# A float32 hybrid decoder layer: order of evacuations, unscaled first products, early output projection, bank-by-bank last tiles, 16-blocks in the triangular inverses

## The chip, the cores and the metric

One core of a Trainium2 chip. The metric is the device time of one launch in microseconds (us); the kernel before takes 2114.07 us (median of three runs, 2109.13 to 2115.06). Engine names are those of the profile: PE (TensorE, matrix products into PSUM), PEld (its weight loads), DVE (VectorE), ACT (ScalarE), POOL (GpSimd), SP (SyncE, which here only issues DMAs). Each engine, and each queue of DMA issues, works its instructions off in the order of the program.

## The reference

One layer on x (1024 tokens, width 1024, float32), three sub-layers with residuals and a norm at the end:

```
x = x + 0.5 * swiglu(rmsnorm(x, g1), w1, w3, w2)        # width 2816: (silu(h@w1) * (h@w3)) @ w2
p = rmsnorm(x, gm) @ w_in                               # 1024 -> 2816
y_rwkv = rwkv7(p[:, :1792])     # 8 heads x 64: S = S*diag(decay) + (S a) b^T + v k^T ;  y = S r
y_gmlp = gelu(pu) * (tril(w_s) @ layernorm(gelu(pv)) + b)  # chunks of 128 tokens
x = x + concat(y_rwkv, y_gmlp) @ w_out
x = x + 0.5 * swiglu(rmsnorm(x, g2), ffn2 weights)
out = rmsnorm(x, gf)
```

rmsnorm divides each token's row by the root of its mean square, then multiplies by a gain per channel. In the rwkv branch b is kk*a, where kk is the key divided by its norm over a head. The recurrence is computed in chunks of 64 tokens; a chunk needs the inverse of a unit triangular 64x64 matrix per head.

## The kernel before, in words

Everything is held transposed: channels on the 128 partitions, 512 tokens (one "row" or "half", 0 and 1) on the free axis. A float32 product is three products of 128x512 on operands that were split into a rounded part and the rest: an ACT cast (L740, L262, L500, L501) and a subtraction on DVE or POOL (L743, L263, L502, L503). The two feed-forward layers use Strassen's scheme of seven products. For the first product, `first_half` (L331) multiplies row 0 (tiles xt) by 22 column tiles of the weights (s = 0 to 21, 24 products each, in two parts); after part 0 the bank is copied out as an intermediate (L352), after part 1 it goes to `gate` (silu, product). `x_build` (L286) makes the combined operands xc from both rows while `first_half` runs; then `up` runs five further products, and `down` (L478) the seven of the third matrix, with `add` (L519, L521) adding each finished PSUM bank into the residual rows rd and res.

A norm's factor per token needs the whole row: `squares` sums squares over the channels, `spread` (L237) has PE sum over partitions, takes the power on POOL, and lets PE spread the factor over the partitions. `apply` (L270) multiplies the row by gain and factor and splits it into xt.

The mixer lies between about 700 and 1435 us. The main stream on PE is w_in, the gmlp part and w_out, one half of the tokens after the other. The rwkv branch is woven into it by `Flow`, which counts a planned time forward with each matrix product and lets a task go on when the planned time has come (`yield 3.0` is a pause of 3 planned us). Per half there are four `pair` tasks (elementwise work of two heads) and four `Oct` objects of 128 tokens (8 octs in all): `prep` (masked score matrices SC), `invert` (inverses of the 8x8 diagonal blocks on DVE, with relayouts through DRAM: ldr, M, tdr, T), `merge` (three levels, blocks of 8, 16, 32 joined by small PE products T,SC / T,X / X,T), `chain` (the state) and `finish`. After the first half's w_out, the second layer's `first_half` starts; at its step 12, or when the rwkv branch is through, `second` (L684) waits for the second half's rwkv results and runs that half's w_out, its norm and then the rest of `first_half`.

The final order on each engine is made by a scheduler that simulates the program; `hp` and `evac` raise priorities in it, and `add_manual_dep` with NoSync adds an order without a wait. Weight tiles go through four buffers raw and four buffers wsp.

Of the kernel before, what the change touches and what calls it, by code (L numbers as in the profile page):

```python
# [45 lines left out]
CON = [("ident", 128), ("me", 128), ("m8", 32), ("m16", 32), ("m32", 32), ("bo", 128), ("cm", 256), ("tri", 128)]  # L46
# [7 lines left out]
def host_constants():  # L54
# [10 lines left out]
        **{f"m{b}": (s64 // (2 * b) == t32 // b) & (s64 // b % 2 == 1) for b in (8, 16, 32)},  # L65
# [82 lines left out]
class K:  # L148
    def __init__(self, ctx, tc, a, out):
# [12 lines left out]
        self.edge = None  # L162
# [28 lines left out]

    def mm(self, *args, **kw):
        i = self.nc.tensor.matmul(*args, **kw)  # L193
        if self.edge is not None:
# [42 lines left out]
    def spread(self, acc, which, wait=1.6):  # L237
# [3 lines left out]
        for kk in range(2):  # L241
            for t in range(4):
                self.rmm(ps[:, t:t + 1], lhsT=sq[:, kk, t * P:(t + 1) * P], rhs=self.one,
                         start=(kk == 0 and t == 0), stop=(kk == 1), skip_group_check=True)
# [25 lines left out]
    def apply(self, dst, res, gain, rb, out=None, ks=range(KT)):  # L270

        nc = self.nc
        for k in ks:
            t = self.xtp.tile([P, HALF], F32, name="silu", bufs=3)
            nc.vector.scalar_tensor_tensor(t, res[k // 2][:, k % 2], self.v(gain, k), rb, op0=ALU.mult, op1=ALU.mult)
# [10 lines left out]
    def x_build(self, pool, xc, src, gain, rb):  # L286
# [15 lines left out]
        for kk in range(4):  # L302
# [10 lines left out]
            yield 3.0  # L313
# [5 lines left out]
            yield 3.0  # L319
# [11 lines left out]
    def first_half(self, xc, ws, hook):  # L331
# [14 lines left out]
        def head(s):  # L346
            wt = self.w_cols(ws[s % 2], s // 2, nc.gpsimd if s % 2 else nc.vector)
            o = self.psum("d")
            yield from prod(wt, o, 0)
            with self.evac():  # L350
                t = new()
                nc.scalar.copy(t, o)  # L352
                nc.sync.dma_start(self.sd[s], t)
            return wt, o

        nxt = yield from head(0)
        for s in range(2 * NP):
            wt, o = nxt
            between = hook(s)
            if s + 1 < 2 * NP and between is None:  # L360
                nxt = yield from head(s + 1)
            yield from prod(wt, o, 1)
            self.gate(us, new, s, 11, o)
            if s % 2:
                nc.sync.dma_start(self.hd[1][s // 2], us.pop(11))
            if between is not None:
                yield from between
                nxt = yield from head(s + 1)
# [109 lines left out]
    def down(self, pool, w2, res, done, loads):  # L478
# [40 lines left out]
        def add(p, bank, row, k):  # L519
            rv = res[row][k // 2][:, k % 2]  # L520
            ve.scalar_tensor_tensor(rv, bank, 0.5, rv, op0=ALU.mult, op1=ALU.add)  # L521
            done(p, row, k)

        for p, y, new, outs in plan:
            if new:
                sets[y] = banks(y)
            for jj in range(NP):
# [18 lines left out]
        for e in late:  # L546
            with self.evac():
                add(*e)

    def build(self, src, gain, w, rb, stats, ready, early=False):  # L550
# [10 lines left out]
        yield from self.x_build(pool, self.xc, src, gain, rb)  # L561
# [25 lines left out]
    def program(self):  # L587
# [17 lines left out]
        rx, rb = yield from self.row_stats(pool, src, "d", 0)  # L605
        x12 = self.halves()
        rbs = []
        self.apply(x12, rx, "g1", rb, self.xn)
        cb.close()
# [5 lines left out]
        flow.spawn(self.build(src, "g1", w1, rbs, stats1, ("xb", 0)))  # L615
        yield from self.first_half(x12, w1, lambda s: None)
# [10 lines left out]
        def task(row):  # L627
            yield 1.0
            rb = yield from self.spread(accs[row], "d" if row == 0 else "e", 2.5)
            if row == 0:  # L630
                rb = self.keep(rb)
                xm[0] = self.halves()
                for k in range(KT):
                    self.apply(xm[0], res[0], "gm", rb, ks=[k])
# [34 lines left out]
        yield ("rwkv", 0)  # L669
        accs = ([], [])  # L670
        out0 = yield from self.w_out(0, xres, accs[0], (self.mp, "h", 3))
        rb = yield from self.spread(accs[0], "e")
        rbs2 = []
        x12 = self.halves()
        self.apply(x12, out0, "g2", rb, self.xn)
# [8 lines left out]
        def second():  # L684
            yield ("rwkv", 1)
            crp.close()
            cm.close()
            p1, c1 = self.open("p1")
            yield from self.w_out(1, xres, accs[1], (p1,))
# [5 lines left out]
            rb1 = yield from self.spread(accs[1], "e")  # L695
            c1.close()
            cxq.close()
            flow.spawn(self.build(xres[1], "g2", w2, rbs2, stats2, ("xb", 1), True))

        yield from self.first_half(x12, w2, hook)  # L700
# [6 lines left out]
        def out(row):  # L707
            yield 1.0
            rb = yield from self.spread(accs[row], "d" if row == 0 else "e", 1.6)
            yield 0.5  # L710
            if row == 0:
                rb = self.keep(rb, pool)
            for k in range(KT):
                with self.hp(0 if row == 0 else PR_EVAC):
                    rv = res[row][k // 2][:, k % 2]
                    nc.vector.scalar_tensor_tensor(rv, rv, self.v("gf", k), rb, op0=ALU.mult, op1=ALU.mult)  # L716
                    (nc.scalar if k % 2 else nc.sync).dma_start(ov[row, k // 2][:, k % 2], rv)
                if row == 0:
                    yield 1.4

        def done2(p, row, k):
            if k % 2 == 0:
                return
            if (row == 0 and (p == 2 or p == 6)) or (row == 1 and p == 7 and k >= 4) or (row == 1 and p == 4):
# [616 lines left out]
```

## Time and profile before

| what | us |
|---|---|
| median of three runs | 2114.07 |
| profiled execution, own time | 2114.52 |
| its span, first to last instruction | 2112.4 |
| PE busy | 1971.0 |
| PEld busy | 1613.1 |
| DVE busy | 1160.4 |
| POOL busy | 975.3 |
| ACT busy | 700.5 |

Busy PE time counts every product from its start to its modelled end; products overlap, so the distance between starts says what one costs. The stages: norm of x to 22 us, first layer's `first_half` and `up` to about 485, `down` to 699, mixer to 1435, second half's w_out to 1489, rest of the second layer.

### The profile page before, as it was taken

Reading aid. Unit: us, or ns where it says so; the run is one execution under the profiler, and the core shown is the slowest. Engines: PE = TensorE matmul, PEld = TensorE weight load, DVE = VectorE, ACT = ScalarE, POOL = GpSimd, SP = SyncE. Lnnn points to the kernel's source line nnn. Section 1 sums busy time; section 2 is a strip of 40 time slices with the busy share of each in tenths; the row PEclk is TensorE's granted clock in tenths of the full one; section 3 lists DMA queues with packets and bytes.
Section 4 is the critical chain, followed back from the end, with each engine's and each line's share of the span. In section 5 each row is a group of like instructions: output and inputs, shape, how many; then the busy total and the mean of one; then the engine's idle time right before and its main releaser. Section 6 shows DMA issues by size and latency. Waiting matters only on the chain. (4 is left out here: it accounts for less than half of the span.)

```text
span 2112.4 us, 34477 instructions
## 1 busy us (share of the span) xinstructions
PE 1971.0 (93%) x13408; PEld 1613.1 (76%) x13408; DVE 1160.4 (55%) x1645; ACT 700.5 (33%) x1205; POOL 975.3 (46%) x749
## 2 busy tenths in 40 slices
PE   6999999998998999999899898997899999999987
PEld 5787888887876778767788777876678888878866
DVE  6716666646658354445534344324756666655576
ACT  5433222223443443241312122233442222224432
POOL 3426665554555565353323133124455666545542
PEclk9999999999999999999999998998899999999998
DMA  8655444447644576553443455435654544476452
GB/s 284 237 165 170 169 159 160 159 149 275 195 151 139 194 242 212 130 203 106 149 132 98 118 157 177 118 126 188 212 175 162 170 168 159 136 264 193 141 178 101
DMA packets 235187, 360.34 MB, mean 171 GB/s; under 512 B 68240, under 2 KB 101008, under 8 KB 235024
## 3 DMA queue, kind: packets, MB, share of 16 engines
q1 hardware_dynamic: 181248, 342.43, 49.0%
q10 hardware_dynamic: 53776, 15.71, 3.2%
q8 instruction: 105, 1.72, 0.3%
q14 instruction: 58, 0.48, 0.1%
HBM read 260.53 MB, written 97.53 MB: 170 GB/s over the span
## 5 line engine op out<-in xcount | busy, mean ns | idle before, releaser
L193 PE MATMUL psd<-xt,wsp 128*128 128x512 f32 x1920 | 490.0, 412 | 12.4 <-ACT silu L352 3.9
L193 PEld LDWEIGHTS psd<-xt,wsp 128*128 128x128 f32 x1920 | 369.3, 196 | 107.2 <-DVE wsp L743 4.9
L743 POOL TENSOR_TENSOR wsp<-raw,wsp 128x512 fp32r<-128x512 f32 x170 | 228.9, 1367 | 363.2 <-ACT wsp L740 353.3
L193 PE MATMUL psd<-xc,wup 128*128 128x512 f32 x1584 | 374.8, 389 | 4.0 <-ACT wup L257 3.6
L193 PE MATMUL psd<-wsp 128*128 128x512 f32 x1440 | 342.6, 397 | 14.1 <-ACT wsp L501 9.5
L193 PEld LDWEIGHTS psd<-xc,wup 128*128 128x128 f32 x1584 | 297.0, 188 | 67.2 <-ACT wup L257 4.5
L193 PEld LDWEIGHTS psd<-wsp 128*128 128x128 f32 x1440 | 271.9, 191 | 77.1 <-ACT wsp L501 11.4
L503 POOL TENSOR_TENSOR wsp<-raw,wsp 128x512 fp32r<-128x512 f32 x154 | 230.1, 1498 | 215.6 <-ACT wsp L501 165.7
L193 PE MATMUL pse<-xc,wup 128*128 128x512 f32 x1056 | 254.4, 389 | 0.0
L258 POOL TENSOR_TENSOR wup<-wraw,wup 128x512 fp32r<-128x512 f32 x132 | 179.0, 1365 | 127.2 <-ACT wup L257 126.2
L193 PEld LDWEIGHTS pse<-xc,wup 128*128 128x128 f32 x1056 | 198.0, 188 | 41.5 <-ACT wup L257 0.5
L740 ACT CAST wsp<-raw 128x512 fp32r<-128x512 f32 x246 | 139.7, 617 | 150.1 <-PE psd L193 98.5
L502 DVE TENSOR_TENSOR wsp<-raw,wsp 128x512 fp32r<-128x512 f32 x110 | 104.9, 966 | 80.1 <-ACT wsp L500 79.9
L385 DVE TENSOR_TENSOR wt<-wraw 128x512 f32<-128x512 f32 x44 | 42.1, 958 | 183.1 <-DMA wraw<-in_ffn_w_dram 183.1
L257 ACT CAST wup<-wraw 128x512 fp32r<-128x512 f32 x132 | 81.3, 619 | 179.4 <-PE psd L193 109.7
L193 PE MATMUL pse<-wsp 128*128 128x512 f32 x396 | 110.1, 406 | 17.2 <-DVE wsp L502 12.7
L500 ACT CAST wsp<-raw 128x512 fp32r<-128x512 f32 x110 | 68.2, 620 | 165.8 <-PE psd L193 65.3
L193 PE MATMUL psc<-wsp 128*128 128x512 f32 x396 | 106.8, 399 | 0.0
L501 ACT CAST wsp<-raw 128x512 fp32r<-128x512 f32 x154 | 94.9, 617 | 32.4 <-DMA raw<-hd 25.7
L193 PEld LDWEIGHTS pse<-wsp 128*128 128x128 f32 x396 | 76.7, 196 | 36.7 <-DVE wsp L502 15.9
L743 DVE TENSOR_TENSOR wsp<-raw,wsp 128x512 fp32r<-128x512 f32 x76 | 60.4, 828 | 69.2 <-ACT wsp L740 56.5
L193 PEld LDWEIGHTS psc<-wsp 128*128 128x128 f32 x396 | 76.5, 194 | 16.4
(225 smaller groups left out, 2509.0 us busy)
## 6 DMA issues: line engine op xcount, KB each, us to landing
wraw<-in_ffn_w_dram SPq DMA_DIRECT2D x88, 512.0 KB, 4.6
raw<-hd SPq DMA_DIRECT2D x154, 256.0 KB, 3.5
raw<-in_ffn_w_dram SPq DMA_DIRECT2D x132, 256.0 KB, 3.2
raw<-in_ffn_w_dram SPq DMA_DIRECT2D x44, 512.0 KB, 4.3
raw<-in_w_in_dram SPq DMA_DIRECT2D x36, 512.0 KB, 4.1
hd<-u SPq DMA_DIRECT2D x66, 256.0 KB, 2.5
hd<-s SPq DMA_DIRECT2D x66, 256.0 KB, 5.0
sd<-silu SPq DMA_DIRECT2D x44, 256.0 KB, 3.4
```

The source lines that it names most:

```text
L193: i = self.nc.tensor.matmul(*args, **kw)
L257: nc.scalar.copy(t[:, 0], src)
L258: eng.tensor_tensor(t[:, 1], src, t[:, 0].bitcast(F32), op=ALU.subtract)
L385: ve.tensor_sub(t1, b12, b11)
L500: nc.scalar.copy(t[:, 0, 0], w)
L501: nc.scalar.copy(t[:, 0, 1], h)
L502: ve.tensor_tensor(t[:, 1, 0], w, t[:, 0, 0].bitcast(F32), op=ALU.subtract)
L503: ge.tensor_tensor(t[:, 1, 1], h, t[:, 0, 1].bitcast(F32), op=ALU.subtract)
L740: self.nc.scalar.copy(dst[:, 0, sl], src[:, sl])
L743: eng.tensor_tensor(dst[:, 1, sl], src[:, sl], dst[:, 0, sl].bitcast(F32), op=ALU.subtract)
```

## The change

1. **Start and first products.** `apply` can run without the factor (rb None). `first_half` runs three heads (part 0 of s = 0 to 2; two in the second layer) on rows that carry only the gain; then the factor comes, and the banks are multiplied by it on the way out: `keep` and the new `gate` multiply on DVE, and POOL multiplies silu's result once more. The scaled rows xn are made later, in `first_build` and `rows`.
2. **Order of evacuations.** `pace` ties an elementwise instruction behind the last main product that was issued; `add` uses it, and takes a bank's uses together.
3. **Early output projection.** `w_out` does its four gmlp tiles first and only then waits for rwkv; `hook` fires when the last chain is through (or at step 17), and the second half's norm and `build` run as a task beside `first_half`.
4. **Last tiles bank by bank.** In product 4 of `down` the last three operand tiles are held and run through one bank after the other; each bank is evacuated behind its own products, and `done2` sums squares tile by tile. Two of the eight last scalings go to POOL.
5. **Inverses from 16-blocks.** `invert` works on 64 partitions with two 8x8 blocks each, joins them to 16x16 on DVE, and `merge` has two levels. The norm of kk is taken per head and chunk (`inv`) and multiplied into SC and Bt; `spread2` and `back2` go.
6. **Relayout DMAs** (ldr, M, tdr, T) are issued by SP, before by ACT. `w_cols` alternates DVE and POOL for the split where POOL did all.

```
+    def pace(self, i):
+        self.tc.add_manual_dep(i.ins, self.last.name, ...NoSync...)
...
     def first_half(...)
+        for s in range(ahead):
+            q.append((yield from head(s)))
+        rb = self.keep((yield from stat))
+        self.flow.spawn(then(rb))
+        for s in range(ahead):
+            keep(s, q[s][1])
...
+        def keep(s, o):
+                nc.vector.tensor_mul(t, o, rb)
+        def gate(s, c):
+                if s % 2 == 0:
+                    nc.vector.tensor_mul(u, c, rb)
+                    nc.scalar.activation(u, u, AF.Silu)
+                    nc.gpsimd.tensor_tensor(u, u, rb, op=ALU.mult)
+                else:
+                    nc.vector.tensor_mul(u, u, c)
...
     def down(...)
-            ve.scalar_tensor_tensor(rv, bank, 0.5, rv, op0=ALU.mult, op1=ALU.add)
+            i = ve.scalar_tensor_tensor(rv, bank, 0.5, rv, op0=ALU.mult, op1=ALU.add)
+            if p != 4:
+                self.pace(i)
...
+                if p == 4 and jj >= NP - 3:
+                    held.append(t)
+                    continue
...
-            for o in outs:
-                for f in range(4):
+            for f in range(4):
+                for o in outs:
                     late.append(...)
+            if p == 4:
+                for f, e in enumerate(late):
+                    for jj, t in enumerate(held):
+                        (the three products of t into bank f)
+                    with self.evac():
+                        add(*e)
...
     def hook(s):
-            if state["done"] or not (("rwkv", 1) in flow.done or s >= 12):
+            if state["done"] or not (("chain", 2 * NO - 1) in flow.done or s >= 17):
...
     def w_out(...)
+                if hf == 0 and n == 4:
+                    yield ("rwkv", half)
+                    sums = ready()
...
     def invert(...)
-        M = self.tl("M", 1, (P, 8, 8))
-        nc.scalar.dma_start(M, self.diag(self.ldr))
+        M = self.tl("M", 1, (64, 16, 16))
+        nc.sync.dma_start(M, self.diag(self.ldr))
...
+        for l, r, o in ((D[:, 0, 0:8, 0:8], M[:, 0:8, 8:16], Z), (Z, D[:, 0, 8:16, 8:16], D[:, 0, 0:8, 8:16])):
+            nc.vector.tensor_mul(tv, l.unsqueeze(2).broadcast_to([64, 8, 8, 8]), ...)
+            nc.vector.tensor_reduce(o, tv, axis=AX.X, op=ALU.add)
...
     def merge(...)
-        for lvl, bs in enumerate((8, 16, 32)):
+        for lvl, bs in enumerate((16, 32)):
...
     def pair(...)
-        ss = self.spread2(sq)
+        for i in range(HALF // CH):
+            for s in HS:
+                self.rmm(ss[s, i:i + 1], lhsT=sq[s, i * CH:(i + 1) * CH], rhs=self.one[s], ...)
-        inv = self.back2(i8)
-        ve.tensor_mul(a, a, inv)
```

How instructions move, at three places. First DVE, where the first layer's `down` goes over from its first product to the next; dt and wsp are operands of coming products, rd and res are evacuations of finished banks. Before:

```order
L502 TENSOR_TENSOR wsp<-raw,wsp 128x512 x7
L493 TENSOR_TENSOR dt<-raw,dt 128x512
L502 TENSOR_TENSOR wsp<-dt,wsp 128x512
L521 SCALAR_TENSOR_TENSOR rd<-psd,rd 128x512 x4
L521 SCALAR_TENSOR_TENSOR res<-psd,res 128x512 x8
L493 TENSOR_TENSOR dt<-raw,dt 128x512 x4
L502 TENSOR_TENSOR wsp<-dt,wsp 128x512 x2
```

Now, with buffer numbers:

```order
L532 TENSOR_TENSOR dt_3816<-raw_4059,dt_3816 128x512
L532 TENSOR_TENSOR dt_3839<-raw_4084,dt_3839 128x512
L541 TENSOR_TENSOR wsp_4060<-dt_3816,wsp_4060 128x512
L560 SCALAR_TENSOR_TENSOR rd_3775<-psd_3781,rd_3775 128x512
L560 SCALAR_TENSOR_TENSOR res_3779<-psd_3781,res_3779 128x512
L560 SCALAR_TENSOR_TENSOR res_3777<-psd_3781,res_3777 128x512
L560 SCALAR_TENSOR_TENSOR rd_3775<-psd_3782,rd_3775 128x512
L532 TENSOR_TENSOR dt_3862<-raw_4107,dt_3862 128x512
L541 TENSOR_TENSOR wsp_4085<-dt_3839,wsp_4085 128x512
L532 TENSOR_TENSOR dt_3885<-raw_4130,dt_3885 128x512
L532 TENSOR_TENSOR dt_3908<-raw_4153,dt_3908 128x512
L560 SCALAR_TENSOR_TENSOR res_3779<-psd_3782,res_3779 128x512
```

Twelve evacuations stood in one block between two operands; now they come three or four at a time between the operands.

Second, PE at the second half's w_out (psd<-wsp) inside the second layer's `first_half` (psd<-xt,wsp); psd<-xc,wup is `up`, pse<-con,Y the last `finish`. Before:

```order
L193 MATMUL psd<-xt,wsp 128x512 x12
L202 MATMUL psc<-WA,SC 64x64 x8
L202 MATMUL pse<-con,Y 64x64 x16
L193 MATMUL psd<-wsp 128x512 x192
L202 MATMUL pse<-one,xs 128x1 x8
L202 MATMUL pse<-con,rr_r 128x128 x4
L193 MATMUL psd<-xt,wsp 128x512 x216
L193 MATMUL psd<-xc,wup 128x512 x2
```

Now:

```order
L200 MATMUL psd<-xt,wsp 128x512 x24
L200 MATMUL psd<-wsp 128x512 x5
L200 MATMUL psd<-xt,wsp 128x512 x12
L200 MATMUL psd<-wsp 128x512 x22
L210 MATMUL pse<-con,Y 64x64 x16
L200 MATMUL psd<-wsp 128x512 x162
L200 MATMUL psd<-xt,wsp 128x512 x3
L210 MATMUL pse<-one,xs 128x1 x8
L200 MATMUL psd<-xt,wsp 128x512 x9
L210 MATMUL pse<-con,rr_r 128x128 x4
L200 MATMUL psd<-xt,wsp 128x512 x108
L200 MATMUL psd<-xc,wup 128x512 x2
```

The last `finish` moves from ahead of w_out into it, and 120 products instead of 216 stand between w_out and `up`.

Third, the relayouts of the first oct. Before, on ACT, among casts and copies:

```order
L1143 DMA ldr_6874<-SC_6841 64x8x64 x2
L1172 DMA M_7045<-ldr_6874 128x8x8
L740 CAST wsp_6774<-raw_6772 128x512 x2
L1158 COPY Bt_6981<-pse_6964 128x512
L1187 DMA tdr0_0_5534<-D_7047 128x8x8
L1187 DMA tdr0_1_5536<-D_7047 128x8x8
L1158 COPY Kt_7000<-pse_6983 128x512
L1191 DMA T_7227<-tdr0_0_5534 64x8x64
L1158 COPY VV_7031<-pse_7014 128x512
L1191 DMA T_7227<-tdr0_0_5534 64x8x64
L1191 DMA T_7227<-tdr0_1_5536 64x8x64 x2
```

Now, on SP, among loads of weights (raw):

```order
L1279 DMA M_7113<-ldr_6989 64x16x16
L1212 DMA oB_7104<-xB0_135 128x4x128
L850 DMA raw_7090<-in_w_in_dram 128x1024
L1212 DMA oK_7106<-xK0_136 128x4x128
L1212 DMA oV_7108<-xV0_137 128x4x128
L1309 DMA tdr0_0_5572<-D_7115 64x16x16
L1309 DMA tdr0_1_5574<-D_7115 64x16x16
L1313 DMA T_7298<-tdr0_0_5572 64x8x64 x2
L1313 DMA T_7298<-tdr0_1_5574 64x8x64 x2
L1245 DMA ldr_7202<-SC_7166 64x8x64 x2
L850 DMA raw_7155<-in_w_in_dram 128x1024
```

The waits of the relayouts for DVE's D and for their own landings now stand in front of SP's loads.

## Rows read from the trace of the kernel before

**Rows 1.** two stretches: length, busy us (instructions) by engine, PEclk, DMA, GB/s
```profile
300.00:400.00 100.00, 100.00 (x443) 82.81 (x442) 59.67 (x82) 27.97 (x47) 61.18 (x46) 1.00 0.51 168
...
700.00:1435.00 735.00, 677.80 (x7839) 557.23 (x7840) 309.65 (x595) 219.27 (x389) 264.39 (x236) 0.94 0.50 151
```

**Rows 2.** PE's waits, whole span: us in total, times, longest
```profile
PE pse L193 <- DVE wsp L502: 12.7, 5, 4.6
PE psd L193 <- ACT wsp L501: 9.5, 4, 7.0
```

**Rows 3.** timeline, start: start, length, instruction, count, [idle before <-releaser]
```profile
4.60 1.06 ACT L231 ACTIVATE xs<-rx 128x1024 f32<-128x1024 f32 x1 [1.65 <-DMA rx<-in_x_dram]
...
21.86 0.62 ACT L262 CAST xt<-silu 128x512 fp32r<-128x512 f32 x1 [1.60 <-DVE silu L275]
...
22.53 4.29 PE L193 MATMUL psd<-xt,wsp 128*128 128x512 f32 x9 [1.49 <-DVE silu L275]
...
29.88 7.27 PE L193 MATMUL psd<-xt,wsp 128*128 128x512 f32 x21
...
37.80 10.52 PE L193 MATMUL psd<-xt,wsp 128*128 128x512 f32 x44
```

**Rows 4.** timeline, two places in the first `down`, one in the second
```profile
500.26 2.07 PE L193 MATMUL pse<-wsp 128*128 128x512 f32 x4 [4.53 <-ACT wsp L500]
...
671.47 27.88 PE L193 MATMUL psd<-wsp 128*128 128x512 f32 x108 [7.03 <-ACT wsp L501]
...
2049.71 1.22 PE L193 MATMUL pse<-wsp 128*128 128x512 f32 x2 [4.64 <-DVE wsp L502]
```

**Rows 5.** timeline, TensorE in the mixer: bursts of small products
```profile
820.21 1.09 PE L202 MATMUL pse<-con,i 128*64 128x128 f32 x16
...
870.60 1.12 PE L202 MATMUL pse<-T,SC 64*64 64x32 f32 x32
871.66 5.16 PE L193 MATMUL psd<-xt,wsp 128*128 128x512 f32 x21
876.75 1.12 PE L202 MATMUL pse<-T,X 64*64 64x32 f32 x32
877.70 1.10 PE L202 MATMUL pse<-X,T 64*64 64x32 f32 x32
```

**Rows 6.** mixer: DMA issues (KB, us to landing), then a wait of SP
```profile
T<-tdr ACTq DMA_DIRECT2D x32, 128.0 KB, 3.5
...
M<-ldr ACTq DMA_DIRECT2D x8, 32.0 KB, 2.8
...
SPq L747 <- POOL wsp L743: 100.0, 31, 12.1
```

**Rows 7.** timeline, from the mixer to the second `up`
```profile
1306.88 1.12 PE L202 MATMUL psc<-S,AR 64*64 64x64 f32 x16 [4.46 <-DVE WA L1245]
...
1433.34 1.98 PE L202 MATMUL pse<-con,Y 64*64 64x64 f32 x32 [8.43 <-POOL Y L1278]
...
1489.56 3.58 PE L202 MATMUL pse<-one,xs 128*128 128x1 f32 x16 [4.27 <-DVE xs L233]
...
1497.21 1.41 DVE L306 SCALAR_TENSOR_TENSOR nx<-nx,vec,rbk 128x512 f32<-128x512 f32 x2 [3.88 <-ACT rbk L283]
...
1505.27 0.68 DVE L263 TENSOR_TENSOR xc<-nx,xc 128x512 fp32r<-128x512 f32 x1
...
1506.47 1.78 DVE L263 TENSOR_TENSOR xc<-nx,xc 128x512 fp32r<-128x512 f32 x1
...
1535.24 1.28 POOL L263 TENSOR_TENSOR xc<-nx,xc 128x512 fp32r<-128x512 f32 x1 [1.28 <-ACT xc L262]
```

**Rows 8.** timeline, end of the span
```profile
2090.03 2.73 DVE L521 SCALAR_TENSOR_TENSOR rd<-psd,rd 128x512 f32<-128x512 f32 x4 [5.65 <-PE psd L193]
...
2096.29 3.57 PE L202 MATMUL pse<-one,xs 128*128 128x1 f32 x16 [4.26 <-DVE xs L233]
...
2103.32 5.36 DVE L716 SCALAR_TENSOR_TENSOR rd<-rd,vec,pse 128x512 f32<-128x512 f32 x8 [3.26 <-PE pse L202]
```

More of the change, by code (lines that the diff above doesn't have):

```diff
@@ L161, in __init__ @@
         self.ws = e(tc.tile_pool(name="ws", bufs=1, reuse_waits="tile"))
-        self.edge = None
+        self.edge = self.last = None
+        self.turns = 0
         base = self.base
@@ L235, in squares, with spread @@
                 acc.append(s)
-    def spread(self, acc, which, wait=1.6):
+    def spread(self, acc, which, wait=1.6, extra=None):
         sq = acc[0]
         ps = self.psum(which)
-        for kk in range(2):
+        parts = [sq[:, 0], sq[:, 1] if extra is None else extra]
+        for kk, x in enumerate(parts):
             for t in range(4):
-                self.rmm(ps[:, t:t + 1], lhsT=sq[:, kk, t * P:(t + 1) * P], rhs=self.one,
+                self.rmm(ps[:, t:t + 1], lhsT=x[:, t * P:(t + 1) * P], rhs=self.one,
                          start=(kk == 0 and t == 0), stop=(kk == 1), skip_group_check=True)
@@ L268, in halves, with apply @@
         return [self.xtp.tile([P, 2, 2, HALF], F32R, name="xt", bufs=4) for _ in range(4)]
-    def apply(self, dst, res, gain, rb, out=None, ks=range(KT)):
+    def apply(self, dst, res, gain, rb, out=None, ks=range(KT), pace=False):
         nc = self.nc
@@ L329, in gate, with first_half @@
                 nc.vector.tensor_mul(us[key], us[key], c)
-    def first_half(self, xc, ws, hook):
+    def first_half(self, xc, ws, hook, stat, then, ahead, wt0=None):
         nc = self.nc
@@ L604, in program, with first_build @@
         pool, cb = self.open("p0")
-        rx, rb = yield from self.row_stats(pool, src, "d", 0)
         x12 = self.halves()
-        rbs = []
-        self.apply(x12, rx, "g1", rb, self.xn)
-        cb.close()
+        rbs, acc0, rx, wt0 = [], [], [], None
+        for kp in range(4):
+            if kp == 2:
+                wt0 = self.w_cols(w1[0], 0, nc.vector)
+            t = pool.tile([P, 2, HALF], F32, name="rx", bufs=4)
+            nc.sync.dma_start(t, src[0][kp])
+            rx.append(t)
+            self.apply(x12, rx, "g1", None, ks=(2 * kp, 2 * kp + 1))
+            self.squares(pool, acc0, t)
+        def first_build(rb):
+            yield 20.0
+            for k in range(KT):
+                t = pool.tile([P, HALF], F32, name="nt", bufs=2)
+                nc.vector.scalar_tensor_tensor(t, rx[k // 2][:, k % 2], self.v("g1", k), rb, op0=ALU.mult, op1=ALU.mult)
+                nc.sync.dma_start(self.xn[k], t)
+                yield 3.0
+            cb.close()
+            yield from self.build(src, "g1", w1, rbs, stats1, ("xb", 0), pace=8.0)
         def stats1(pool):
@@ L693, in stats2 @@
                 rbs2.append(self.keep(rb1, pool))
[L695 to L700, printed above, removed]
+            yield from self.build(xres[1], "g2", w2, rbs2, stats2, ("xb", 1), True)
+        yield from self.first_half(x12, w2, hook, self.spread(accs[0], "e"), rows, 2)
         yield from self.rest(w2, ("xb", 1), cxt.close)
@@ L764, in dense_T, with w_out @@
         return o
-    def w_out(self, half, xres, acc, sums):
+    def w_out(self, half, xres, acc, ready, x12=None):
         nc = self.nc
@@ L830, in mixer_consts @@
         nc.gpsimd.memset(self.S, 0.0)
+        self.inv = [mp.tile([P, PR, HALF // CH], F32, name=f"inv{h}") for h in range(2)]
         self.pcc = [mp.tile([P, PR, HALF // CH], F32, name=f"pcc{h}") for h in range(2)]
@@ L1212, in merge @@
             pt = K_.psum("e", (P, 2, NB, CH // 2))
-            for n in range(1 if lvl == 2 else 2):
+            for n in range(1 if lvl == 1 else 2):
                 for b in range(NB):
```

237 lines of the change are left out of this document (152 added, 85 removed).

## The prediction

> **What bounds the kernel now.** I read stretches first, then PE's waits, then the timeline at each place where one ends. In the stretch from 300 to 400 us PE starts 443 products of 128x512, one per 0.226 us, and is busy all the time at a granted clock of 1.00 [rows 1]: there nothing but fewer products could help, and the change takes none of these away. In the mixer (700 to 1435) PE is still busy 677.8 of 735 us, but with 7839 instructions at a clock of 0.94 [rows 1]: many are small, and each removed one is time on the path. PE's waits name the rest: the products of `down` wait for operand splits, 12.7 and 9.5 us [rows 2]. The timeline then shows the start, two places of `down`, the mixer, the second w_out and the end [rows 3, 4, 5, 7, 8]. So the kernel is bound by PE, and the question is what each part takes from PE's stream or from its gaps.
>
> The sum is made against the profiled execution (2114.5 us, span 2112.4), which lies 0.45 us above the median: the same number for this purpose. By repetition 0.3%, 6 us, is what can be told from no change.
>
> **Start.** Before, the first products wait for the norm: 9 start at 22.53, 21 at 29.88, and the steady stream only at 37.80 (44 in 10.52 us, 0.239 each) [rows 3]. Now they need the gain alone, but the statistic queues behind other work: on ACT four squares of 1.06 and eight casts of 0.62 (rows and first weights) from 4.60 on, to about 13.8 [rows 3], then a DVE addition of 1024 columns (twice the 0.68 of 512 [rows 7]), so 15.1. The partition sums take 3.58 [rows 7] and the way from their start to the first use of the factor 7.0 (2096.29 to 2103.32 [rows 8]). In PE's order 46 products stand before the factor's spreading, 32 of them behind the sums: 18.7 + 32 x 0.226 = 26, or 33 if they run at half clock. With the second row's sums (3.6) 48 products are done by 30 to 37; before, the 48th starts at 37.80 + 18 x 0.239 = 42.1. Gain 5 to 12; I take 9, and keep 2 to 15, since evacuations now go over DVE and a POOL product.
>
> **Evacuations in `down`.** At 500.26, 671.47 and 2049.71 PE has waited 4.53, 7.03 and 4.64 us for a split [rows 4], each time because DVE had a block of evacuations or final scalings in front of the operand. The order rows show that block of twelve cut into threes and fours. Four-bank blocks remain at product 4 with fewer operands ahead, so I don't count all: of the 22.2 us of the two wait lines and the 4.5 of the first place [rows 2, 4] three quarters, 18 net of what shifts. Bounds 6 (only the first place) and 30 (all, with the slow products behind it).
>
> What such a wait costs is seen at 671.47: the 108 products behind it take 27.88 us, 3.5 more than 108 x 0.226 = 24.4 [rows 1, 4]. The Trainium skill (TensorE: Matmul & The Clock Gate, HAM oscillation) says that an idle gap throttles the array and that what follows runs cold; by that rule the trace agrees, and a removed 7 us gap would be worth 10.5. My sum leaves this out except in the bound of 30.
>
> **Mixer, products removed.** One merge level per oct goes: T,SC, T,X and X,T, 32 instructions each. Start to start such a burst costs 1.06 (870.60 to 871.66) and 0.95 (876.75 to 877.70) [rows 5], so 3.0 per oct and 24 for eight. `back2` was 16 instructions per pair, 820.21 to about 821.2, 1.0 each: 8 for eight pairs. `spread2`'s eight are replaced by 32 of one column per pair; the trace has no such product, the nearest are the 32 of 32 columns at 1.0. I take old and new as equal. Together 32. Bounds: 12, if most of the freed time turns into waiting for the recurrence, and 45, if waits inside the bursts go too. What is added lies on DVE: per oct two products and two reductions of 512 elements, at 0.68 each 2.7 us [rows 7], against a DVE that is busy 309.65 of 735 [rows 1]; a merge level with its two evacuations is taken out of the same latency. At nothing, as long as DVE's idle half covers it.
>
> **Relayouts on SP.** ACT loses waits, SP gets them. SP then stands per oct until ldr has landed (about 2.8, as M), M has (2.8), D is there (some 6 of DVE by the row lengths above), tdr and T follow (about 3 and 3.5) [rows 6]: an estimate of 15 us in which a weight load behind it doesn't go out. Four raw buffers cover that: the mixer loads 82 weight tiles in 735 us (five rows of the DMA issues there, 35 + 13 + 24 + 8 + 2), 9 us each, so 36 us of stock, and SP's longest wait is for buffers to come free (100.0 us in 31 times [rows 6]), so it is ahead. I take -4 (ACT's casts come earlier), bounds -15 and +20.
>
> **Second w_out.** Three gaps of PE: 4.46 behind the first half's w_out, with DVE at applying the factor (now applied late), 8.43 for the last `finish` (now inside w_out), 4.27 for the sum of squares [rows 7]. Of the last 0.7 is covered by the three products ahead of it, the others go: -13. Against it stands the build of xc. It ran from 1497.21 to 1535.24 + 1.28, 39.3 us, under 216 products [rows 7]; now 120 stand between w_out and `up`. From w_out's last product PE comes to `up` after 120 x 0.226 + 3.6 of wait + 3.6 of sums + about 2 of spreading = 36; the build begins after 3.6 + 0.7 + 7.0 = 11 and ends at 50, its first-needed operands some 4 sooner. So PE waits about 10: bounds 0 and 20. Sum for this place: -3.
>
> **End.** Before: last additions from 2090.03 for 2.73, the sums 2096.29, the scalings 2103.32 for 5.36 [rows 8]. Now three banks are added and squared under the next bank's products; behind the last there is one addition (0.68), half a square and half of the sums (1.8 saved), and six scalings instead of eight (1.3 saved). From the last addition to the sums 3.5 shrink to about 0.6: 2.9 + 1.8 + 1.3 = 6, bounds 3 and 8.
>
> **Sum.** 9 + 18 + 32 + 4 + 3 + 6 = 72 less: 2114.5 - 72 = 2042.5, so 2043 us.
>
> **Rivals.**
> *The freed mixer time isn't returned.* The recurrence goes oct by oct, and `invert` has longer planned pauses (7, 2, 9 for 4, 2.4 and 6). Against it: the main stream has no tie to the octs until w_out, and PE's idle share is small there [rows 1]. With 12 of 32 returned and DVE as the later releaser, 2063 to 2075.
> *DVE and POOL hold each other up in the two `first_half`.* A subtraction takes 0.68 and, beside POOL, 1.78 [rows 7]; new are a DVE evacuation and POOL's product per two steps. If the second build takes ten more and evacuations hold the banks, 15 to 25 on top: 2058 to 2068. The Trainium skill (SBUF — State Buffer, Who interferes with whom) gives the rule: a DVE instruction with two SBUF inputs and a reading GpSimd one exclude each other, one with a single SBUF input doesn't contend. By it the new evacuations (one input from PSUM) stay free and only the build's additions suffer; the 1.78 agrees.
> *More than counted.* All gaps of `down` go with their slow tails (30), the waits in the merges too (45), and the build is in time: 12 + 13 + 10 further, about 2005 to 2015.
> *Slower: SP runs dry.* If SP stands over 36 us per oct, because D waits in DVE's queue and T's landing behind it, weight loads come too late and PE stops: beyond that point 12 to 15 us for each of eight octs, some 110 against 72 gained: about 2150. For it: the second oct's ldr already stands in front of a load in the order rows. Against: the estimate of 15.
> *The parts do nothing*, since `down` and the build find new waits as large: 2110.
>
> **How the numbers follow.** Forecast 0.53 (own range 2023 to 2063), time not returned 0.16, DVE and POOL 0.10, more than counted 0.13, SP dry 0.05, nothing 0.03. The range 2003 to 2088 holds all of the first three and most of the fourth, over 8 in 10. Faster by over 0.3%: 0.92 less a small part for surprises in these, 0.91; within: 0.03; slower: 0.06.
>
> **What would show it.** Steady products before 30 us; no wait over 3 us of PE for a split of `down`; 256 instructions less in T,SC and T,X each and in X,T, with the mixer about 30 us shorter; no wait before pse<-con,Y but one before the first psd<-xc,wup; last product to end of span about 15 us instead of 20. I am wrong if PE's busy time falls but its idle time grows by as much, or if SP's waits for D and T are followed by PE waits for weights.

## The result

The changed kernel takes 2098.03 us (median of five runs, 2096.19 to 2104.43), the kernel before 2111.25 (five runs beside it). The ratio is 0.9934, 95% interval 0.9912 to 0.9957: faster by 13 to 14 us, where 72 were forecast. The profiled execution has a span of 2095.0 us against 2112.4.

By the first product of each stage on PE (where `up` goes over into `down`, by the last product of `up`), and the clock of the whole execution:

| stretch of the profile, us | before | after | difference | forecast |
|---|---|---|---|---|
| start to the first `up` | 160.9 | 167.2 | +6.3 | -9 |
| first `up` | 302.2 | 303.6 | +1.4 | 0 |
| first `down` | 239.5 | 240.7 | +1.2 | -18 for both |
| mixer, w_out, `first_half` to the second `up` | 855.4 | 838.0 | -17.4 | -39 |
| second `up` | 302.1 | 305.0 | +2.9 | 0 |
| second `down` | 231.5 | 223.7 | -7.8 | see above |
| its last product to the end of the span | 20.7 | 16.8 | -3.9 | -6 |

```profile
core 0: 2112.4 us, clock 0.962
```

for the span and mean granted clock before, and after:

```profile
core 0: 2095.0 us, clock 0.953
```

### The profile page after: what moved, and what is told of

Same layout as the page of the kernel before. It is cut to its first block, busy times and chain, and to the rows that moved or that the text cites. A ratio compares the mean times of both kernels' runs of the same rounds, so it can differ in the third digit from the quotient of the medians.

```text
span 2095.0 us, 33201 instructions
## 1 busy us (share of the span) xinstructions
PE 1937.4 (92%) x12704; PEld 1587.4 (76%) x12704; DVE 1281.4 (61%) x1819; ACT 677.3 (32%) x1159; POOL 977.4 (47%) x736
## 5 line engine op out<-in xcount | busy, mean ns | idle before, releaser
L200 PE MATMUL psd<-xt,wsp 128*128 128x512 f32 x1920 | 494.3, 415 | 36.9 <-DVE silu L372 16.8
L200 PEld LDWEIGHTS psd<-xt,wsp 128*128 128x128 f32 x1920 | 376.5, 200 | 126.9 <-DVE silu L372 13.1
L542 POOL TENSOR_TENSOR wsp<-raw,wsp 128x512 fp32r<-128x512 f32 x154 | 232.1, 1514 | 192.3 <-ACT wsp L540 157.7
L846 POOL TENSOR_TENSOR wsp<-raw,wsp 128x512 fp32r<-128x512 f32 x134 | 187.5, 1415 | 251.0 <-ACT wsp L843 250.7
L541 DVE TENSOR_TENSOR wsp<-raw,wsp 128x512 fp32r<-128x512 f32 x110 | 107.3, 986 | 58.1 <-ACT wsp L539 57.8
L846 DVE TENSOR_TENSOR wsp<-raw,wsp 128x512 fp32r<-128x512 f32 x112 | 93.9, 871 | 56.1 <-ACT wsp L843 55.9
L200 PE MATMUL pse<-wsp 128*128 128x512 f32 x396 | 105.3, 393 | 3.1 <-DVE wsp L541 2.6
L540 ACT CAST wsp<-raw 128x512 fp32r<-128x512 f32 x154 | 94.8, 617 | 16.8 <-DMA raw<-hd 14.7
L200 PEld LDWEIGHTS pse<-wsp 128*128 128x128 f32 x396 | 73.2, 188 | 22.2 <-DVE wsp L541 6.5
```

Of the source, the lines that this page charges most:

```text
L540: nc.scalar.copy(t[:, 0, 1], h)
L541: ve.tensor_tensor(t[:, 1, 0], w, t[:, 0, 0].bitcast(F32), op=ALU.subtract)
L542: ge.tensor_tensor(t[:, 1, 1], h, t[:, 0, 1].bitcast(F32), op=ALU.subtract)
L846: eng.tensor_tensor(dst[:, 1, sl], src[:, sl], dst[:, 0, sl].bitcast(F32), op=ALU.subtract)
```

## The profile after

**The start** came as forecast. TensorE's timeline of the changed kernel (start, length, instruction, count, [idle before <-releaser]), to answer [rows 3]:

```profile
10.10 1.22 PE L200 MATMUL psd<-xt,wsp 128*128 128x512 f32 x2 [10.10 <-ACT wsp L843]
12.34 5.49 PE L200 MATMUL psd<-xt,wsp 128*128 128x512 f32 x12 [1.02 <-DVE wsp L846]
20.52 2.65 PE L210 MATMUL pse<-one,xs 128*128 128x1 f32 x16 [2.69 <-DVE xs L241]
23.03 10.06 PE L200 MATMUL psd<-xt,wsp 128*128 128x512 f32 x32
...
33.74 0.71 PE L200 MATMUL psd<-xt,wsp 128*128 128x512 f32 x2
34.29 1.84 PE L210 MATMUL pse<-one,xs 128*128 128x1 f32 x16
```

The 48th product is done at 34.5 and the second row's sums at 36.1, where before the 48th ended at 42.1 (37.80 + 18 x 0.239 [rows 3]): 6 to 8 us gained, 9 forecast.

**It is lost again before `up`.** The stretch from the first product to the first `up`, with length, busy us (instructions) of PE, PEld, DVE, ACT, POOL, granted clock, DMA share, GB/s. Before:

```profile
22.00:161.00 139.00, 133.87 (x553) 107.00 (x553) 77.44 (x91) 62.08 (x113) 55.14 (x39) 0.99 0.62 205
```

and after:

```profile
10.00:167.00 157.00, 138.30 (x576) 110.64 (x576) 112.72 (x135) 57.58 (x97) 77.31 (x52) 0.95 0.63 214
```

DVE is busy 35 us more, POOL 22 more, PE idle 19 us instead of 5, and the clock is 0.95 instead of 0.99. What PE waits for, in the whole span (us in total, times, longest), to answer [rows 2]:

```profile
PE psd L200 <- DVE silu L372: 16.8, 6, 6.7
PE psd L200 <- ACT wsp L843: 15.4, 2, 10.1
PE psd L200 <- ACT wup L266: 12.8, 2, 11.0
PE pse L210 <- DVE oG L1408: 12.0, 3, 5.9
PE psd L200 <- ACT wsp L540: 10.4, 4, 5.0
```

The first line is `keep`, the evacuation that now multiplies by the factor. The kernel before waits once for its copy on ACT, 3.9 us in the second layer, and never in the first. Here is the longest one of the first layer, on all engines' timeline:

```profile
155.40 0.69 DVE L424 TENSOR_TENSOR wt<-wraw 128x512 f32<-128x512 f32 x1 [5.96 <-DMA wraw<-in_ffn_w_dram]
156.01 0.68 DVE L384 TENSOR_TENSOR silu<-silu,psd 128x512 f32<-128x512 f32 x1
...
159.49 0.68 DVE L372 TENSOR_TENSOR silu<-psd,rbk 128x512 f32<-128x512 f32 x1
160.09 0.68 DVE L424 TENSOR_TENSOR wt<-wraw 128x512 f32<-128x512 f32 x1
160.32 5.13 PE L200 MATMUL psd<-xt,wsp 128*128 128x512 f32 x12 [6.18 <-DVE silu L372]
```

DVE stands 5.96 us for a weight load of `up`; the evacuation that holds the bank is queued behind it and five more instructions. DVE had such a wait before too (5.4 us for the same load), but the copies then stood in ACT's queue, and PE waited for none of them there. And the twelve products behind the gap take 5.13 us, 0.43 each instead of 0.226 [rows 1]: the granted clock from 160 to 165 us is 0.51, the lower of its two levels (1.2 and 2.4 GHz).

**The second `first_half`**, with w_out inside it, waits for the last `finish`, for a bank and for the build of xc:

```profile
1454.48 1.98 ACT L843 CAST wsp<-raw 128x512 fp32r<-128x512 f32 x3 [3.93 <-DMA raw<-yr]
1455.15 34.53 PE L200 MATMUL psd<-wsp 128*128 128x512 f32 x144 [5.30 <-ACT wsp L843]
...
1529.07 5.15 PE L200 MATMUL psd<-xt,wsp 128*128 128x512 f32 x12 [6.68 <-DVE silu L372]
...
1549.44 1.22 PE L200 MATMUL psd<-xc,wup 128*128 128x512 f32 x2 [11.04 <-ACT wup L266]
```

The result of `finish` comes back through DRAM (tile yr), so moving `finish` into w_out turned 8.43 us of waiting into 5.30. At the bank wait DVE is not idle but busy with the build: two scalings and a split took 5.2 us beside POOL. The forecast had the build of xc done 50 us after w_out's last product and PE there after 36, so a wait of 10. `up` starts after 60 (1489.3 to 1549.4): the build began 3.5 us later than forecast and took 47 us instead of 39, and PE came after 49, with 6.7 us of bank waits on the way. That the wait is 11, close to the forecast 10, is luck: both sides came later.

**The mixer** with all up to the second `up`, before:

```profile
702.00:1558.00 856.00, 784.97 (x8273) 642.99 (x8273) 382.23 (x678) 269.02 (x477) 318.19 (x274) 0.93 0.52 158
```

after:

```profile
711.00:1549.00 838.00, 752.25 (x7568) 620.43 (x7568) 469.74 (x810) 253.85 (x447) 296.00 (x249) 0.92 0.53 163
```

From the last `finish` to the second `up` alone, before and after:

```profile
1435.30:1558.00 122.70, 106.87 (x435) 85.58 (x433) 74.47 (x85) 51.58 (x90) 53.99 (x38) 0.91 0.61 207
1444.40:1549.40 105.00, 77.26 (x339) 62.66 (x338) 78.14 (x85) 41.74 (x71) 52.53 (x36) 0.86 0.64 217
```

In the whole stretch 705 products are gone and PE is busy 33 us less, though at a lower clock; but it idles 86 us instead of 71. DVE has 87 us more, of which I had counted 22.

**In `down`** the waits of [rows 4] are smaller, not gone:

```profile
674.91 8.27 PE L200 MATMUL psd<-wsp 128*128 128x512 f32 x24 [4.99 <-ACT wsp L540]
685.38 1.19 PE L200 MATMUL psd<-wsp 128*128 128x512 f32 x4 [2.20 <-ACT wsp L540]
...
2047.82 22.57 PE L200 MATMUL psd<-wsp 128*128 128x512 f32 x91 [3.35 <-DVE wsp L541]
```

**The end**, to answer [rows 8]:

```profile
2078.57 0.69 DVE L560 SCALAR_TENSOR_TENSOR rd<-psd,rd 128x512 f32<-128x512 f32 x1
...
2079.92 1.05 PE L210 MATMUL pse<-one,xs 128*128 128x1 f32 x8 [1.38 <-DVE xs L814]
...
2085.93 4.04 DVE L798 SCALAR_TENSOR_TENSOR rd<-rd,vec,pse 128x512 f32<-128x512 f32 x6 [3.88 <-ACT rbk L298]
2085.98 2.50 POOL L793 TENSOR_TENSOR rd<-rd,rbk 128x512 f32<-128x512 f32 x2 [2.83 <-ACT rbk L298]
```

From the last addition to the sums there are 0.7 us where 3.5 were; the scalings start 6.7 us behind its end, before 10.6.

## The experiments

Ratios are to the kernel before, run on the same chip beside each; the changed kernel's is 0.9934 (0.9912 to 0.9957). 0.005 are about 10 us.

**One part taken back or moved.** The mixer's weight splits on POOL alone:

```
     def w_cols(...)
-            eng = self.nc.vector if self.turns else self.nc.gpsimd
+            eng = self.nc.gpsimd
```

> The changed kernel, but the weight tiles of the mixer that it splits by turns on DVE and POOL are all split on POOL again (35 us less on DVE in the mixer, 35 x 1.4/0.8 = about 55 more on POOL). DVE theory (the products taken out of the mixer came back as waits because DVE got later: 396 us busy there instead of 310): the mixer, 733.8 us in the profile of the changed kernel, becomes 8 to 20 us shorter, the whole about 2080 to 2090. Rival, recurrence theory (the octs' latency sets the stage, whoever does the splits): within 4 us. Rival, POOL theory (its 1.4 us splits are the later ones): 5 to 15 us longer.

Measured 2080.82 us, ratio 0.9845 (0.9798 to 0.9892). At that point it looked like the DVE theory; the run pace7 below takes this reading away.

The intermediate copied by ACT and scaled on POOL:

```
-                nc.vector.tensor_mul(t, o, rb)
+                nc.scalar.copy(t, o)
+                nc.gpsimd.tensor_tensor(t, t, rb, op=ALU.mult)
```

> The changed kernel, but the intermediate of the two first_half is copied out of its bank by ACT (unscaled) and multiplied by the factor on POOL from SBUF, where DVE did it from the bank. DVE theory (banks are held because their evacuation stands in DVE's queue behind the build of xc): the first layer's first_half, 157.1 us in the profile, loses 10 to 15 us, and the second's 104.1 us stretch some 6; the whole 2080 to 2088. Rival, POOL theory (22 more POOL products of 1.4 us beside DVE slow the build of xc itself, and up waits for it): the waits for banks go but up's wait grows by as much, 2095 to 2105.

Measured 2101.56, ratio 0.9952 (0.9934 to 0.997), in the range of the POOL theory. The first `up` starts at 173.8, 6.6 us later still:

```profile
10.00:174.00 164.00, 137.50 (x577) 111.26 (x578) 112.65 (x112) 68.99 (x120) 109.30 (x73) 0.92 0.61 208
```

POOL is busy 32 us more, and DVE not less although it has 23 instructions fewer: the ones that are left take longer. So the reading that fits is that not DVE's queue alone but DVE and POOL together are the bound here.

The second factor of silu's result on DVE instead of POOL:

```
-                    nc.gpsimd.tensor_tensor(u, u, rb, op=ALU.mult)
+                    nc.vector.tensor_mul(u, u, rb)
```

> The changed kernel with the second factor of silu's result multiplied on DVE (11 instructions a layer, 0.68 us if nothing disturbs) where POOL did it in 1.4 to 1.8. POOL theory (POOL's reading products hold up DVE's two-operand ones, 1.7 us instead of 0.68, and delay its splits): first_half of the first layer, 157.1 us, 4 to 8 us shorter. DVE queue theory (every instruction more on DVE delays the banks): 4 to 8 us longer. The whole accordingly 2090 to 2095 or 2102 to 2108.

Measured 2080.09, ratio 0.9847 (0.9817 to 0.9878). `up` starts at 161.8, 5.4 us earlier, as the POOL theory has it, but then waits for its weights (6.5 us for a split on DVE): the first `down` starts at 473.5 against 470.8. Moving the work between the two engines moves the wait; the 18 us in the whole don't come from this place. The profile has 17 us less from the mixer to the second `up`.

Both `first_half` on scaled rows, as before:

```
-        out0 = yield from self.w_out(0, xres, accs[0], lambda: (self.mp, "h", 3), x12)
+        out0 = yield from self.w_out(0, xres, accs[0], lambda: (self.mp, "h", 3))
+        rb = yield from self.spread(accs[0], "e")
+        self.apply(x12, out0, "g2", rb, self.xn)
...
-                nc.vector.tensor_mul(t, o, rb)
+                nc.scalar.copy(t, o)
```

and the same for the first layer; `gate` leaves out the factor too. With the scaled rows the first layer's build also starts earlier and with shorter planned pauses (3 us, where the changed kernel has 8).

> The changed kernel, but both first_half run on scaled rows as before (factor awaited at the start and after the first half's w_out, intermediates copied by ACT, no factor on the way out); all else stays. DVE theory (the evacuations with the factor hold the banks and delay the build of xc): the first up starts at 161, 6 us earlier than the 167.2 of the changed kernel, with the 12 us lost at the start given back behind it; the second first_half gains some 10 us before up against 4 to 6 lost behind w_out; the whole 8 to 14 us shorter, 2084 to 2090. Rival (unscaled first products are worth their 9 us, as forecast, and the waits have another cause): 6 to 14 us longer, 2104 to 2112.

Measured 2076.06, ratio 0.9836 (0.9804 to 0.9869). The first `up` starts at 158.7:

```profile
22.00:159.00 137.00, 131.32 (x553) 107.43 (x554) 77.42 (x91) 62.20 (x113) 55.43 (x39) 0.99 0.63 208
```

All five other builds with scaled rows in the first layer, the kernel before among them, have it at 158.5 to 161.9 us, all eight other builds that share the changed kernel's unscaled evacuations there at 166.3 to 168.6. The unscaled products, 9 us of my gains, cost 4 to 10 us in the first layer. The build's pauses were not altered alone by as much; 7 planned us in place of 8 (pace7 below) leave `up` at 166.9. In the second layer, with 168 products between w_out and `up` in both cases, `up` starts 18.0 us later than these products alone would need, in hook14 (unscaled) 25.8; this is one profile of each.

More cover for the second build:

```
-            if state["done"] or not (("chain", 2 * NO - 1) in flow.done or s >= 17):
+            if state["done"] or not (("chain", 2 * NO - 1) in flow.done or s >= 14):
```

> The changed kernel with the second w_out allowed from step 14 of first_half on instead of 17 (it came at 16, with the last chain): 168 products instead of 120 stand between it and up, as cover for the build of xc. Cover theory (up waits 11 us because the build has too little cover): the 11.0 us wait before up goes, 6 to 12 us shorter, 2086 to 2092. Rival (the products taken from under the last chain and finish are missed there as much): waits for chain and finish grow by 8 to 20 us, 2098 to 2108. Rival, DVE theory (the build is limited by DVE, which the evacuations share, however long the cover): under 4 us gained.

Measured 2096.41, ratio 0.992 (0.9892 to 0.9947): the changed kernel's time. With 48 products more the wait before `up` is still there, since the build is the slower side, and the last `finish` is waited for longer (the second line; ACT's cast waits for raw<-yr, 9.0 us):

```profile
PE psd L200 <- ACT wup L266: 10.4, 1, 10.4
PE psd L200 <- ACT wsp L843: 9.3, 1, 9.3
```

Evacuations in the order of before:

```
     def pace(self, i):
+        return
...
-            for f in range(4):
-                for o in outs:
+            for o in outs:
+                for f in range(4):
```

> The changed kernel without the ordering of the evacuations (the tie to the last main product goes, and the banks' uses stand in the order of before). Forecast of before (ordering saves 18 us in the two down): 12 to 20 us longer, 2110 to 2118. Rival (the profile shows the first down no shorter than before, 240.7 against 239.5 us, and the second 7.8 shorter of which the last tiles may be all): within 5 us of the changed kernel, 2095 to 2103.

Measured 2090.73, ratio 0.9897 (0.9862 to 0.9932): shorter, not longer. Yet both `down` are longer, 247.1 and 232.7 us against 240.7 and 223.7, and the 4.5 us wait of [rows 4] is back:

```profile
PE psd L200 <- ACT wsp L540: 8.0, 2, 6.1
PE pse L200 <- ACT wsp L539: 4.5, 1, 4.5
```

So the ordering is worth 15 us in `down`, about my 18, and 20 us were gained between the mixer and the second `up`, where no instruction stands that this edit touches.

The last tiles of `down` and the end as before:

```
-                if p == 4 and jj >= NP - 3:
+                if False:
```

with the end's sums and scalings of before.

> The changed kernel with the last tiles of both down run tile by tile as before, evacuated together, and with the end (sums, scalings) of before. Forecast (bank by bank saves 6 at the end, nothing elsewhere): the stretch from the last product of down to the end of the span 4 to 6 us longer, the first down unchanged: 2102 to 2105. Rival (holding three operands back costs in the first down, which came out 16 us longer than ordering alone would leave it): first down 4 to 10 us shorter, the end 4 to 6 longer, the whole within 5 us of 2098.

Measured 2095.57, ratio 0.9919 (0.9894 to 0.9944). The end is 4.1 us longer (21.0 us from the last product), and the first `down` 3.6 us longer, so no cost of holding back three operands is seen. The whole is not longer than the changed kernel's, but a difference of this size is within what another order may do (see pace7).

The relayouts on ACT:

```
-        nc.sync.dma_start(M, self.diag(self.ldr))
+        nc.scalar.dma_start(M, self.diag(self.ldr))
```

and so for ldr, tdr and T.

> The changed kernel with ldr, M, tdr and T issued by ACT again. Forecast (SP is free enough, ACT gains a little): mixer within 8 us, 2098 to 2106. SP theory (the relayouts wait in SP's order behind weight loads and hold these up; the rest of the change made the mixer with 8-blocks 42 us longer than before, and this is its largest candidate): the mixer 15 to 35 us shorter, 2063 to 2083. ACT theory (relayouts on ACT hold up casts of weights): 8 to 20 us longer.

Measured 2106.05, ratio 0.9962 (0.9935 to 0.9988). The SP theory falls: the whole is 8 us longer, not shorter. The stretch from the mixer to the second `up` is 14 us longer in the profile, which is of the slowest of ten executions (2119.55).

**The 16-blocks from both sides.** Taken out of the changed kernel:

```
     def merge(...)
-        for lvl, bs in enumerate((16, 32)):
+        for lvl, bs in enumerate((8, 16, 32)):
```

with `invert` and `diag` of before.

> The changed kernel with the inverses and the three merge levels of before (8x8 blocks on 128 partitions, 128 more T,SC, T,X products and 128 X,T per half as before); the rest of the change stays, relayouts on SP too. Counted term (24 us of PE products are really saved): the mixer becomes 20 to 28 us longer, the whole 2118 to 2126. DVE theory (what PE saves is spent again waiting for DVE, which got 5 us more work per oct): only 3 to 12 us longer, 2101 to 2110. Latency theory (the 16-blocks lengthen each oct's path): it gets shorter, 2085 to 2095.

Measured 2137.43, ratio 1.0113 (1.0067 to 1.0159): 39 us longer, more than the 20 to 28 of the counted term.

And put alone into the kernel before (the same lines the other way round):

> The kernel before with nothing changed but the inverses from 16-blocks (two merge levels). Counted term: 24 us of products less, 2085 to 2092. By the run with 8-blocks in the changed kernel, where the third level cost 39: 2070 to 2080. Latency rival (a longer path per oct eats the gain where nothing else is changed): 2100 to 2115.

Measured 2090.95, ratio 0.9904 (0.9877 to 0.9931): 20 us, my counted 24. With 39 us in the other direction, no theory by which the 16-blocks don't pay is left; how much they pay is known no closer than these two, since each edit also brings another order.

The norm of kk as before (`spread2`, `back2`; SC masked in one instruction, Bt copied by ACT):

```
-        self.Bt, self.Kt = self.turned("Bt", B, inv[:, :, self.c0:self.c0 + NC]), self.turned("Kt", Kt)
+        self.Bt, self.Kt = self.turned("Bt", B), self.turned("Kt", Kt)
...
+        inv = self.back2(i8)
...
+        ve.tensor_mul(a, a, inv)
```

> The changed kernel with the norm of kk multiplied into the rows as before (spread2, back2 and one product on a), SC masked in one instruction and Bt copied by ACT; 16-blocks stay. Counted term (8 us of back2 products, their replacement free): 6 to 10 us longer, 2104 to 2108. DVE theory (four maskings per bank instead of one and Bt on DVE cost more than back2): 3 to 10 us shorter, 2088 to 2095.

Measured 2089.91, ratio 0.9892 (0.9867 to 0.9917): 8 us shorter, as the DVE theory has it, but see pace7 next.

**The order in the mixer.** By now no_pace and gate_dve, which touch nothing in the mixer itself, had made the stretch from there to the second `up` 17 to 21 us shorter. So one planning number was altered, and no work:

```
-            yield from self.build(src, "g1", w1, rbs, stats1, ("xb", 0), pace=8.0)
+            yield from self.build(src, "g1", w1, rbs, stats1, ("xb", 0), pace=7.0)
```

> The changed kernel with nothing but one planning number altered: the pause between two steps of the first layer's build of xc, 7 planned us instead of 8. No work changes; the order in the mixer, which the scheduler forms anew, does. Reshuffle theory (the mixer's 734 us is the luck of one order; half of what wcols_pool, no_pace and gate_dve gained there is such luck): the mixer becomes 8 to 20 us shorter, the granted clock rises, 2080 to 2092. Rival (those gains belong to the edits): within 4 us of 2098.

Measured 2082.98, ratio 0.9833 (0.9811 to 0.9854): 15 us from no work at all (21 by the ratios). From the mixer to the second `up`:

```profile
709.00:1537.00 828.00, 730.70 (x7569) 603.64 (x7570) 474.35 (x811) 254.93 (x450) 299.67 (x249) 0.94 0.54 167
```

Against the row of the changed kernel above: the same products, DVE 5 us busier, PE idle even 11 us more, but PE busy 22 us less, at a granted clock of 0.94 instead of 0.92. So 11 us of the stretch come with the order, and PE's time shows them as clock. The gains of wcols_pool, gate_dve and inv_before in this stretch (10, 17 and 11 us) are of about the size that this run has without them, so they prove nothing about their edits.

**Together.** The edits of scaled12 and wcols_pool:

> Both losses taken out of the changed kernel at once: scaled rows in both first_half and the mixer's weight splits on POOL alone. If the two are separate (22 and 17 us in the medians of the single runs): 2098 less 30 to 40, 2058 to 2068. If they are one cause counted twice (POOL's and DVE's load in the mixer and behind it): no better than the better of the two, 2072 to 2082.

Measured 2071.0, ratio 0.9801 (0.977 to 0.9832): between the two ranges expected. Those of scaled12 and inv_before:

> Scaled rows in both first_half and the norm of kk as before; 16-blocks, ordering of evacuations, early w_out, last tiles and relayouts on SP of the change stay. If the two gains (22 and 8 us) add: 2066 to 2071. If the second was reshuffle: 2073 to 2082.

Measured 2070.68, ratio 0.9784 (0.9766 to 0.9802): in the range for two gains that add, but 5 us under scaled12 is less than an order may bring. And of all three:

> As best2, and the mixer's weight splits on POOL alone. If DVE's load in the mixer counts: 4 to 10 us under best2. If it doesn't: equal within 4 us.

Measured 2071.99, ratio 0.9788 (0.9762 to 0.9814): no difference, so no cost of DVE's load by the splits is seen. All three are faster than both kernels, by 26 us or more than the changed one, and not to be told from one another.

## Why the prediction was wrong

**Start, and the price of the unscaled products.** "I take 9, and keep 2 to 15, since evacuations now go over DVE and a POOL product." The 6 to 8 us at the start are there; the step that failed is that the evacuations were priced at nothing in the sum. They are 33 DVE and 11 POOL instructions and 8 row scalings, beside a build of xc that these two engines set the pace of. Scaled rows give 8.5 us at the first `up`, 1.4 in it and 7.8 before the second: 18 us, which with the 9 forecast is a miss of some 27. (Against it stand some 2.5 us: scaled12 waits 3.5 us behind the first half's w_out, the changed kernel 1.0.) This is firm for the first layer (6 builds against 9); the 7.8 rest on one pair. This was my second rival, with a chance of 0.10; I had priced it by the second layer's build alone, and its 15 to 25 us were about the size.

**Second w_out.** "The build begins after 3.6 + 0.7 + 7.0 = 11 and ends at 50": it ends at 60. The 39.3 us of before were taken as the build's own length; it shares DVE and POOL with the new evacuations, and takes 46 (1503.8 to 1549.4). A wait of 10 was right only because of the 6.7 us that PE lost on the way.

**The clock.** The sum priced a gap at its length and a product at its length at full clock. Over 44 runs of the unchanged kernel before, the time goes from 2104.4 at a mean clock of 0.966 to 2126.2 at 0.957, about 17 us per 0.01 (correlation -0.83). The changed kernel's five runs have a mean of 0.950, against 0.961: by that slope some 18 us, which nothing in my sum held, and nothing in the change was meant to move. It is a correlation over repeated runs, and no term of its own: the slow products behind the new waits are part of it, so it overlaps with the 27. pace7 shows that the order alone brings more than half of it back (0.957). The Trainium skill (TensorE: Matmul & The Clock Gate, HAM oscillation) has a gap followed by cold products; the 12 products in 5.13 us behind 6.18 us of waiting agree, and the kernel before pays for it too. What I had left out, as a bound of one place in `down`, belongs into every term that adds a wait of several us.

**Mixer.** The count was right: 705 products less, 20 us for the 16-blocks alone in the kernel before. What hid it in the changed kernel is 15 us more idle time and the clock. Of the 15, 12 lie between the last `finish` and `up`, where PE idles 27.7 of 105.0 us (before 15.8 of 122.7, with its 8.43 ahead of that stretch): the term of the second w_out, -3 in the sum, counted neither the way of `finish` through DRAM nor the longer build nor the banks. Which instruction of the mixer's order makes one order better than another stays open: pace7 waits longer than the changed kernel and is faster. DVE got 87 us more in this stretch (I had overlooked `w_cols`, by which its splits go from 22.1 to 57.3 us), but wcols_pool, best3 and combo1 show no cost of it that stands out from the scatter of orders.

**Evacuations in `down`.** "Of the 22.2 us ... three quarters": taking the order back costs 6.4 and 9.0 us, 15 in place of 18. That the first `down` is none the shorter against before is not explained by it: without the order it is 247.1, 8 us above before, and a part of that is the clock (0.95 there, 0.97 before and in the changed kernel). What lowered the clock was not tried. In the four builds that have the order and scaled rows the first `down` takes 236.2 to 239.8 us, so some of the loss seems to come with the unscaled rows.

**Relayouts and end.** -4 was forecast for the relayouts: on ACT the whole is 8 us longer, within what an order may do. The end gave 3.9 of 6: the three savings are there as counted, but the factor's copy by ACT now stands ahead of the scalings (0.6), and behind the last of them on DVE the end is 5.0 us away instead of 3.7.

"More than counted" and "SP runs dry" did not happen; "the freed mixer time isn't returned" did for a part, by the clock; whether waits for the recurrence had a share is not separated (PE stands 12.0 us for its oG, 4.6 before).

## What to carry to other kernels

An evacuation that moves to another engine takes over everything that stands in that engine's queue, its waits for loads too: price it by what is queued ahead of it, not by its length. Where a scheduler forms the order anew, measure an edit against a second order of the same work before believing its time, and look at the stages that the edit touches; here one planning number, with no work behind it, was worth 15 us. In a kernel that PE bounds, a wait of several us costs more than its length: here 12 products behind 6.18 us took 5.13 us instead of 2.7.

## What was not expected of the hardware

DVE can be shut out for a whole run of POOL instructions, not only for one. Setting up the mixer's constants, of 14 elements per partition, took 0.17 us in scaled12, 1.33 in the kernel before beside POOL's memsets, and now, beside POOL's queue that runs through to 702.5:

```profile
695.64 6.92 DVE L914 TENSOR_SCALAR vconst<-vec 128x14 f32<-128x14 f32 x1
...
698.91 1.28 POOL L542 TENSOR_TENSOR wsp<-raw,wsp 128x512 fp32r<-128x512 f32 x1
700.15 2.37 POOL L912 TENSOR_TENSOR wT<-wT,con 128x1024 f32<-128x1024 f32 x1
```

Instructions that read PSUM were not slowed. In the first layer's `first_half` (busy us, mean ns, idle before):

```profile
L372 DVE TENSOR_TENSOR silu<-psd,rbk 128x512 f32<-128x512 f32 x22 | 14.9, 683 | 13.5 <-PE psd L200 10.0 <-ACT rbk L298 3.5
L272 DVE TENSOR_TENSOR xc<-nx,xc 128x512 fp32r<-128x512 f32 x10 | 10.0, 1008 | 0.0
L321 DVE SCALAR_TENSOR_TENSOR nx<-nx,vec,rbk 128x512 f32<-128x512 f32 x8 | 9.3, 1182 | 1.5 <-ACT rbk L298 1.5
```

All are 128x512 with two tensor inputs; with both in SBUF one takes 1.0 to 1.2 us on the mean, beside POOL, with one in PSUM it keeps 0.68, as the Trainium skill (SBUF — State Buffer, Who interferes with whom) has it for a single SBUF input outside DVE's two-port modes. The constants above have a single SBUF input too, and came out only when POOL's run ended; so the prediction's short form of the rule, without that condition, says too much. The evacuations themselves are not slowed; they are queued behind instructions that are.
